# Scatter of the experts' outputs in fp32r with an exact one-hot and a split y, one expert later, and one more weight buffer

## The chip, the cores and the metric

The kernel runs on one core of one Trainium2 chip. The metric is the device time of one execution in microseconds (us); three executions of the kernel before took 1401.58, 1402.41 and 1404.16 us (median 1402.41).

## What is computed

The program is three transformer layers over 256 tokens of 1024 features: a retention layer and a stick-breaking attention layer, each with a gated feed-forward, and then a layer with two mixers and a mixture of experts. The change lies in the last part, cut here to what matters:

```
hn2 = rms_norm(x, g_norm2) * (1 + scale2) + shift2
ffn = hierarchical_moe(hn2, ...)      # 4 groups x 8 experts; top-1 group, top-2 experts in it
#   per expert e, on the tokens routed to it:
#   y = (silu(xb @ w_gate[e]) * (xb @ w_up[e])) @ w_down[e]     # 1024 -> 512 -> 1024
#   out[token] += y_row * weight(token, choice)
x = x + gate2 * ffn
return rms_norm(x, g_final)
```

All is in fp32. The 32 experts' weights are 6 MB each, 192 MB of the 374.68 MB that the program moves.

## The kernel before

**The experts' stage** (`experts`, from 898.60 us of the span to its end) goes over the 32 experts in order. Each expert has 64 slots for tokens. Two experts make a pair: the x of a pair's 128 slots is gathered at once, and the y of its 128 slots is scattered at once. TensorE (PE) does for expert e, in this order:

- `gate_up` (L1717): 32 products of 64 slots, moving 512 weights each; ScalarE (ACT) then takes the silu into `h` (L1721) and VectorE (DVE) multiplies by the up half (L1722).
- `down` of the expert before, e - 1 (L1747): 8 records of products, then the transposes of `h` of expert e (`turn`, L1729), then 8 more. DVE then copies the transposes to `hT` (L1733), which is one buffer that the `down` products still read, and takes y out of PSUM times the layer's gate (L1753), in two halves of 64 partitions, to one half of `Y`.
- where e is odd, `gather` (L1696) of the next pair: one-hot products of x into two PSUM tiles; ACT takes the first four blocks of 128 features to `xg` (L1708), DVE the last four (L1706). The next `gate_up` reads them block by block.
- where e is even and not 0, `sc` of the pair that is then complete (L1832): four full-size fp32 products `accs[t][j] += S[j]^T Y[j]`, S being a [128 slots, 256 tokens] matrix that holds a token's routing weight where the token sits in the slot. S is made on DVE at the start of an odd expert, by `slots` (L1759, L1761), ahead of the one-hot for the gather, `hot` (L1660 to L1667).

In the first expert's turns the last steps of the routing (`route_rest`) are put in between: rows of slot positions and of weights (`rowsb`) come at expert 1, behind the gather.

**The weights' ring.** `Stream` keeps a plan of all 1 MB chunks of weights in the order of their use and issues their DMAs on the SyncE queue (L131) into a ring of buffers; a chunk's DMA is issued as soon as a buffer is released, which PE's last product on the old chunk does. The ring has `RING` = 10 buffers from the start, gets three more of small tiles' memory and others later, and five at the start of the experts' stage. DMAs of constants go by the GpSimd (POOL) queue, which uses a scratch region of SBUF.

**Numbers in fp32r.** Elsewhere in the kernel an fp32 product is made as three fp32r products of split operands; `hilo` (L363, L364; for weights L153, L156) makes such a split: ACT copies to `hi` (rounded to fp32r), DVE subtracts to get `lo`.

Of the kernel before, what the change touches and what calls it, by code (L numbers as in the profile page):

```python
# [21 lines left out]
T = 256  # L22
NT = 2
D = 1024
# [8 lines left out]
RING = 10  # L33
# [9 lines left out]
# the modulation's chunks in the gaps of the first phase and at the four boundaries  # L43
MODS = 6, 5, 5, 6, 10
AHEAD = 6
# the order of the mixers' steps, each with its head or part
# [12 lines left out]
class Blocks:  # L59
    """[:, KC, :] in two tiles of four blocks each."""  # L60
# [12 lines left out]
class Half:  # L73
    """A split half of a chunk; [a:b] gives its (hi, lo) columns, inside a quarter of the chunk."""
# [11 lines left out]
class Stream:  # L86
    """Weights in chunks of up to [128, 2048], in the order of their use; quarters of some are split for fp32r."""
# [11 lines left out]
    def extend(self, pool, tag, bufs, n):  # L99
        """n more buffers, filled before the ones of now come round again."""  # L100
        k = (self.nd - self.at) % len(self.slots)
        self.slots = [(pool, tag, bufs)] * n + self.slots[k:] + self.slots[:k]
        self.at = self.nd
        self.free += n
        self.keep = False
        self.fill()
# [5 lines left out]
    def more(self, n=1):  # L112
        """n of the ring's buffers that had been in use for other things."""
        pool, tag, bufs = self.slots[0]
        self.extend(pool, tag, bufs, n)

    def spare(self):
        """A buffer that no chunk needs any more."""
        assert self.nd >= len(self.plan) and self.free > 0
        t = self.buffer()  # L120
        self.nd += 1
        self.free -= 1
        return t
# [43 lines left out]
    def later(self, *steps):  # L167
        """Steps of other work, one after each quarter that is used."""
        self.todo.extend(steps)
# [7 lines left out]
    def half(self, name):  # L177
        """The next split half."""
# [5 lines left out]
    def chunk(self, name):  # L184
        """The next chunk that is used as it is; release() follows its last use."""
# [8 lines left out]
class Body:  # L194
    # classes of tiles: columns, dtype, and buffers by phase
# [4 lines left out]
    def __init__(self, ctx, tc, a, upto=99):  # L200
# [19 lines left out]
        # small tiles in buffers of the ring, which come to the stream of weights later  # L220
        self.slabs = {}
        for cls, n in (("rot", 2), ("k2", 1)):
            t = [ringp.tile([128, 2048], F32, tag="ring", name="slab", bufs=RING + SLABS) for _ in range(n)]
            self.slabs[cls] = [x[:, o:o + 512] for x in t for o in range(0, 2048, 512)][:6], itertools.count()
            # and 1024 columns more, or all
# [3 lines left out]
    def plan(self):  # L229
# [12 lines left out]
        def bound(i, name, arr):  # L242
            """The modulation's chunks of a boundary with the phase's first one among them."""
# [43 lines left out]
    # ---- tiles  # L287
# [4 lines left out]
    def phase(self, name, **bufs):  # L292
        """A pool for the tiles of a phase, in the place of the last one's."""
# [10 lines left out]
    def view(self, cls, shape, name):  # L304
        """A tile of a class, seen as shape."""
# [19 lines left out]
    def a(self, name="a"):  # L325
        """One of the other four banks."""
        return self.psa.tile([128, 512], F32, tag="a", name=name, bufs=4)

    def banks(self, name):
        """A pool on the four other banks, in the place of the last one's."""  # L330
# [13 lines left out]
    def gain(self, src):  # L344
        """A row of D gains on every partition."""
# [8 lines left out]
    # ---- products  # L354
# [6 lines left out]
    def hilo(self, hi, lo, src):  # L361
        """hi + lo = src, for fp32r."""
# [3 lines left out]
    def transpose4(self, src, c0, name="tr", p=None):  # L366
        """Four blocks of 128 columns of src, transposed."""
# [5 lines left out]
    def natural(self, name, xT, evac):  # L373
        """x @ the next two chunks: [128 tokens, 512] for each tile of tokens."""
# [16 lines left out]
    def transposed(self, name, xT, outs, split=False):  # L391
        """Each out [128 features, 256 tokens] = (x @ the next half)^T; split: tokens of the first tile first."""
# [14 lines left out]
    def rows(self, name, yT, accs, first, last, gate=None, amid=None, begun=None):  # L407
        """accs[t][half] += y[:, two blocks of rows] @ the next chunk; yT[i]: [128, 256] of a block of rows.
        After the last one x gets the sums, and the norm that follows begins; amid: two things on the way;
        begun: the weights of the last one, the first two of their blocks used but for one part."""  # L410
# [55 lines left out]
    def sums1(self, h):  # L466
        """A half of the second tile of tokens of x gets its sums."""
# [3 lines left out]
    # ---- norms  # L471
    def add_x(self, t, h, s, gate=None, square=True):
        """A half of x += s (times a gate), and the sum of its squares."""
# [16 lines left out]
    def rms(self, ss, r=None):  # L490
        """The rms of rows with the sums of squares ss of their halves."""
# [17 lines left out]
    def rsqrt(self, s, n, sign=False, eng=None):  # L509
        """(s / n + EPS) ** -0.5 of one or two columns, on the vector engine alone; negative if sign."""  # L510
# [24 lines left out]
    def to_xT(self, t, h, p, lo):  # L535
        """A half of x^T of a tile of tokens, split: its hi or its lo."""
# [7 lines left out]
    def xT(self):  # L544
        """hi and lo of [128, KC, T]."""
# [4 lines left out]
    def plain_norm(self):  # L550
        """The norm of x that follows some rows: chain(t) after the sums, in steps; join(n) goes on from there,
        on the tensor engine with n products of the modulation."""
# [36 lines left out]
    def boundary(self, i):  # L589
        """The rest of the norm of x, which becomes transposed and split, and products of the modulation."""  # L590
# [14 lines left out]
    # ---- modulation: a quarter of silu(c) @ w_ada + b_ada; rows 32 g of its tile hold 384 columns each  # L605
    def ada(self, i, cls="nat", eng=None):
        """The biases of the quarters that a boundary completes, which get the products."""
# [5 lines left out]
    def ada_steps(self):  # L613
        nc = self.nc
        for s in range(4):
            p = self.w("ada")
            for kc in range(KC):
# [5 lines left out]
                if kc == KC - 1:  # L623
# [3 lines left out]
                    if s == 1:  # L627
                        # by way of memory, for the gate on every partition
# [4 lines left out]
    def ada_columns(self, s, m):  # L633
# [4 lines left out]
        # modc[:, 12 s + 3 g + j] = columns 1536 s + 384 g + 128 j ...  # L638
# [3 lines left out]
    def spread(self, s, t):  # L642
        """t = columns 512 .. 1535 of an odd quarter on every partition."""
# [10 lines left out]
    def setup(self):  # L654
# [22 lines left out]
        for _ in range(WARM):  # L677
            # the tensor engine's clock goes up
            nc.tensor.matmul(p, zero[:, 0:128], zero, start=True, stop=True)
        # the first gain, a row on every partition  # L680
# [45 lines left out]
    # ---- retention  # L726
    def rotary(self, p):
        """The rotated halves of p [128, 512], split."""
# [75 lines left out]
    def conv_taps(self, u, p, cws, n):  # L804
        """u[:, c, :] = the causal convolution of p[:, c T:c T + T] with n taps, the bias last in cws[c]."""
# [9 lines left out]
    # ---- gated feed-forward with the causal convolution  # L815
# [28 lines left out]
    # ---- attention helpers  # L844
    def qk_split(self, b):
        """q / 8 and k of b, split."""
# [9 lines left out]
    # ---- stick-breaking attention  # L856
    def stick(self, xT):
# [20 lines left out]
        def v2(p):  # L878
            """Values of two pairs of heads."""
# [90 lines left out]
    # ---- the second block's mixers  # L970
    def affine(self, out, p, h, A, B, js):
        """out[:, j, :] = a block of p * A + B, by partitions."""
# [8 lines left out]
    def entry_norm(self):  # L981
        """x = the first block's norm of x, x / r * g; then the second block's first norm, modulated: that of x g times
        (mean((x g)^2) + EPS r^2)^-0.5, as r^2 = mean(x^2) + EPS."""
# [20 lines left out]
        def chain(t):  # L1004
            # the squares of x and of x g of both halves, but for the last of these, h
# [15 lines left out]
        def chain0(t):  # L1021
            # Pool has the first half of x g, the other one is there before
# [62 lines left out]
    def halve(self):  # L1085
        """sigmoid(x) = (tanh(x / 2) + 1) / 2"""
# [4 lines left out]
    def mixers(self, xT):  # L1091
# [4 lines left out]
        # of the second tile of tokens; of the first the part from 128  # L1096
# [15 lines left out]
        def gates_post():  # L1112
# [5 lines left out]
            # log_sigmoid(f)  # L1118
# [7 lines left out]
        # a part of vm in the rest of a slab  # L1126
# [23 lines left out]
        def qkm_post(h):  # L1150
            u, s = S.pop(("u", h)), {}

            def silu():
                # u is a half of the convolution: silu = (tanh(u) + 1) u
# [8 lines left out]
            # decays  # L1163
# [85 lines left out]
        def ml3(h, late=False):  # L1249
            """h and its norm over the head."""  # L1250
# [68 lines left out]
        def mo3(i):  # L1319
            """Two heads, transposed."""  # L1320
# [11 lines left out]
        def yt(i):  # L1332
            """Rows of the head and of the pair of heads i, transposed and split."""
# [12 lines left out]
        def wout(i):  # L1346
            if not S.get("accs"):
                S["accs"] = self.accs()
            for j in range(2):
                st.keep = i == 1  # L1350
                self.rows("mix", [[z[:, 2 * i + j, :] for z in yT]], S["accs"], i + j == 0, False)
                if i + j == 2:
                    # the first four blocks of y have been used
# [3 lines left out]
        def begin(k):  # L1357
            """A part of the last rows, their first two blocks."""
# [42 lines left out]
    # ---- experts  # L1401
    def open_experts(self):
        """The experts' tiles take the place of the mixers', and more buffers for weights."""
# [699 lines left out]
```

## Time and profile before

| what | value |
|---|---|
| median of three executions | 1402.41 us |
| the profiled execution: span from its first to its last instruction | 1400.5 us |
| PE busy | 1366.5 us, 98% of the span |
| DVE, ACT, POOL busy | 58%, 43%, 4% |
| granted TensorE clock, mean | 0.996 |
| moved by DMA | 374.68 MB, mean 268 GB/s |
| of it software DMA (POOL's) | 3.54 MB |

The profiled execution's time is known by its span, which lies 1.9 us under the median of the three timed executions. Busy shares are of the whole span; the stages differ (in the experts' stage ACT is at about a tenth and DVE at a third, while the DMA engines are busy all the time), so the prediction reads the stage by itself. A matmul's duration in the profile is longer than the distance to the next one, since matmuls are pipelined; costs on PE are therefore read from distances of starts. An fp32 product is two records; the products of 64 slots run two at a time on halves of the array's columns.

### The profile page before, as it was taken

Reading aid. Unit: us, or ns where it says so; the run is one execution under the profiler, and the core shown is the slowest. Engines: PE = TensorE matmul, PEld = TensorE weight load, DVE = VectorE, ACT = ScalarE, POOL = GpSimd, SP = SyncE. Lnnn points to the kernel's source line nnn. Section 1 sums busy time; section 2 is a strip of 40 time slices with the busy share of each in tenths; the row PEclk is TensorE's granted clock in tenths of the full one; section 3 lists DMA queues with packets and bytes.
Section 4 is the critical chain, followed back from the end, with each engine's and each line's share of the span. In section 5 each row is a group of like instructions: output and inputs, shape, how many; then the busy total and the mean of one; then the engine's idle time right before and its main releaser. Section 6 shows DMA issues by size and latency. Waiting matters only on the chain. (4 is left out here: it accounts for less than half of the span.)

```text
span 1400.5 us, 21543 instructions
## 1 busy us (share of the span) xinstructions
PE 1366.5 (98%) x8332; PEld 999.6 (71%) x8332; DVE 815.8 (58%) x1734; ACT 596.4 (43%) x1187; POOL 60.1 (4%) x117
## 2 busy tenths in 40 slices
PE   9999999999999999999999999999999999999997
PEld 7888878999989998999996898743444334334432
DVE  6767758777775666877777787534233233333323
ACT  5555546566666776666556666410010000000101
POOL 0000000000010001000003122000000000000000
PEclk9999999999999999999999999999999999999999
DMA  9655368544465226654449536899999999999940
GB/s 365 280 186 183 139 235 358 193 184 181 145 257 221 91 76 259 270 183 185 170 143 381 220 128 242 339 398 406 371 411 413 406 416 413 406 403 418 413 183 31
DMA packets 56859, 374.68 MB, mean 268 GB/s; under 512 B 7085, under 2 KB 7905, under 8 KB 15666
## 3 DMA queue, kind: packets, MB, share of 16 engines
q1 hardware_dynamic: 55440, 369.66, 67.8%
q0 software_dynamic: 1168, 3.54, 0.7%
q8 instruction: 66, 1.08, 0.3%
q14 instruction: 39, 0.32, 0.1%
q10 hardware_dynamic: 146, 0.07, 0.0%
HBM read 372.19 MB, written 1.05 MB: 267 GB/s over the span
## 5 line engine op out<-in xcount | busy, mean ns | idle before, releaser
L156 DVE TENSOR_TENSOR lo<-ring,hi 128x512 fp32r<-128x512 f32 x519 | 335.1, 688 | 101.1 <-ACT hi L153 95.2
L153 ACT ACTIVATE hi<-ring 128x512 fp32r<-128x512 f32 x519 | 300.7, 623 | 120.3 <-PE nat_ps L359 41.2
L1717 PE MATMUL gu<-ring,xg 128*64 128x512 f32 x984 | 219.1, 596 | 0.4 <-PEq L1771 0.4
L357 PE MATMUL up<-xT,hi 128*128 128x256 f32 x704 | 199.8, 284 | 0.0
L359 PE MATMUL up<-xT,lo 128*128 128x256 f32 x704 | 199.6, 283 | 0.0
L358 PE MATMUL up<-xT,hi 128*128 128x256 f32 x704 | 199.5, 283 | 0.0
L1721 ACT ACTIVATE h<-gu 64x512 f32<-64x512 f32 x32 | 18.8, 588 | 355.5 <-PE gu L1717 355.5
L1717 PEld LDWEIGHTS gu<-ring,xg 128*64 128x64 f32 x984 | 68.3, 137 | 134.9 <-issue 131.7
L357 PEld LDWEIGHTS up<-xT,hi 128*128 128x128 f32 x704 | 134.2, 191 | 2.0 <-issue 1.2
L358 PEld LDWEIGHTS up<-xT,hi 128*128 128x128 f32 x704 | 134.1, 191 | 0.8
L359 PEld LDWEIGHTS up<-xT,lo 128*128 128x128 f32 x704 | 134.2, 191 | 0.0
L1722 DVE TENSOR_TENSOR h<-h,gu 64x512 f32<-64x512 f32 x32 | 22.1, 691 | 178.0 <-ACT h L1721 178.0
L1747 PE MATMUL y<-ring,hT 128*64 128x512 f32 x480 | 114.7, 599 | 0.5 <-DVE hT L1733 0.5
L812 DVE SCALAR_TENSOR_TENSOR slab<-up,conv,slab 128x254 f32<-128x254 f32 (+1 forms) x176 | 72.7, 476 | 25.7 <-ACT slab L808 25.2
L1832 PE MATMUL acc<-Y,S 128*128 128x512 f32 x128 | 59.2, 606 | 19.3 <-DVE Y L1753 19.3
L1747 PEld LDWEIGHTS y<-ring,hT 128*64 128x64 f32 x480 | 31.7, 136 | 53.6 <-issue 48.1
L357 PE MATMUL nat_ps<-hi,xT 128*128 128x512 f32 x176 | 69.3, 394 | 0.0
L359 PE MATMUL acc<-hi,slab 128*128 128x512 f32 x176 | 69.2, 393 | 0.0
L1696 PEld LDWEIGHTS xg<-goh,x 128*128 128x128 f32 x512 | 60.1, 196 | 12.5 <-issue 12.2
L357 PE MATMUL acc<-hi,slab 128*128 128x512 f32 x176 | 69.0, 392 | 0.0
L358 PE MATMUL acc<-lo,slab 128*128 128x512 f32 x176 | 68.8, 391 | 0.0
L359 PE MATMUL nat_ps<-hi,xT 128*128 128x512 f32 x176 | 68.7, 391 | 0.0
(434 smaller groups left out, 2432.0 us busy)
## 6 DMA issues: line engine op xcount, KB each, us to landing
ring<-gu SPq DMA_DIRECT2D x123, 1024.0 KB, 9.5
ring<-dn SPq DMA_DIRECT2D x59, 1024.0 KB, 8.2
ring<-ffn_u SPq DMA_DIRECT2D x44, 1024.0 KB, 4.8
ring<-ada SPq DMA_DIRECT2D x32, 768.0 KB, 4.4
ring<-ret_w SPq DMA_DIRECT2D x22, 1024.0 KB, 10.3
ring<-ffn_d SPq DMA_DIRECT2D x22, 1024.0 KB, 5.0
ring<-sb SPq DMA_DIRECT2D x12, 1024.0 KB, 6.1
ring<-ret_o SPq DMA_DIRECT2D x8, 1024.0 KB, 7.8
```

The lines of the kernel that those rows point to most:

```text
L153: self.nc.scalar.activation(hi, src, AF.Copy)
L156: (eng or self.nc.vector).tensor_tensor(lo, src, hi.bitcast(F32), op=ALU.subtract)
L357: mm(out, l[0], r[0], start=start, stop=False, **k)
L358: mm(out, l[0], r[1], start=False, stop=False, **k)
L359: mm(out, l[1], r[0], start=False, stop=stop, **k)
L812: nc.vector.scalar_tensor_tensor(u[:, c, s:], p[:, c * T:c * T + T - s], cw[:, n - 1 - s:n - s], u[:, c, s:], op0=ALU.mult, op1=ALU.add)
L1696: self.nc.tensor.matmul(p[:, j * n:j * n + n], self.x[:, t, kc * 128:kc * 128 + 128], oh[:, t, :], start=t + j == 0, stop=t + j == NT + 2, ...
L1717: nc.tensor.matmul(p[64 * i:64 * i + 64, :], xs(kc), raw[:, i * 512:i * 512 + 512], start=kc == 0, stop=kc == KC - 1)
L1721: nc.scalar.activation(h[64:128, :], p[0:64, :], AF.Silu)
L1722: nc.vector.tensor_tensor(h[64:128, :], h[64:128, :], p[64:128, :], op=ALU.mult)
L1747: nc.tensor.matmul(p[64 * i:64 * i + 64, :], hT[:, c, :], raw[:, h * 512:h * 512 + 512], start=c == 0, stop=c == 3)
L1832: nc.tensor.matmul(accs[t][j], S[p][j][:, t * 128:t * 128 + 128], Y[0][:, j, :], start=p == 0, stop=p == E // 2 - 1, skip_group_check=True)
```

## The change

1. `RING` is 11 instead of 10. The memory comes from POOL's DMA scratch, which is set to 2048 bytes of a partition. (Two more things take the rest: a second Y tile, and four S buffers instead of two.)
2. `slot_rows` replaces `scatter_rows` for the pairs: S becomes the exact one-hot (1 where the token sits in the slot) in fp32r, and the slot's weight goes into a column `ws`, [128, 1], summed up by the first operation's accumulator. That is three DVE operations for each S where there were two.
3. y comes out of PSUM times the slot's weight and times the gate into `f` (a `scalar_tensor_tensor`), and `hilo` splits `f` into `Yh` and `Yl`, both fp32r. This happens in each of the two halves: a DVE operation, an ACT copy, a DVE subtraction.
4. `sc` is eight fp32r products (hi and lo for each of four) in the place of four fp32 ones.
5. `sc(q - 1)` comes in the odd expert after the pair, between its `gate_up` and the `down` of the even expert; before, it stood one expert earlier, behind the `down` that completed the pair. The last `sc` stays at the end.
6. At expert 1 the two steps of the routing that make `rowsb`, and the first `slots`, come ahead of the first `down`, as its evacuation needs `ws`.

```diff
-RING = 10
+RING = 11
+SCRATCH = 2048
...
     def down(self, hT, chunks, odd, evac, mid=None):
...
         for i in (odd, 1 - odd):
-            out = outs[i]
             r, h = slice(64 * i, 64 * i + 64), i ^ odd
-            nc.vector.tensor_tensor(out, p[r, :], self.gate2[r, h * 512:h * 512 + 512], op=ALU.mult)
+            evac(i, r, h, p[r, :])
...
+    def slot_rows(self, idx):
+        V, rows, wts = self.nc.vector, *self.rowsb
+        u = self.mp.tile([128, 2 * T], F32, tag="k2", name="su", bufs=2)
+        w = self.mp.tile([128, 1], F32, tag="ws", name="ws", bufs=4)
+        V.scalar_tensor_tensor(u, rows, idx, wts, op0=ALU.is_equal, op1=ALU.mult, accum_out=w)
+        v = self.mp.tile([128, T], F32, tag="k2", name="sv", bufs=2)
+        V.tensor_scalar(v, rows[:, T:], idx, None, op0=ALU.is_equal)
+        s = self.mp.tile([128, T], F32R, tag="S", name="S", bufs=4)
+        V.scalar_tensor_tensor(s, rows[:, 0:T], idx, v, op0=ALU.is_equal, op1=ALU.add)
+        return s, w
...
         def dn(e, mid=None):
...
-                Y[0] = mp.tile([128, 2, 512], F32, tag="Y", name="Y", bufs=1)
-            self.down(hTs.pop(e), stream("dn"), o, [Y[0][0:64, o, :], Y[0][64:128, 1 - o, :]], mid)
+                Y[e // 2] = [mp.tile([128, 2, 512], F32R, tag=n, name="Y" + x, bufs=1) for n, x in (("Y", "h"), ("Yl", "l"))]
+            hi, lo = Y[e // 2]
+            def evac(i, r, h, p):
+                f = mp.tile([128, 512], F32, tag="k2", name="y", bufs=2)
+                nc.vector.scalar_tensor_tensor(f[r, :], p, S[e // 2][h][1][r, :], self.gate2[r, h * 512:h * 512 + 512],
+                                               op0=ALU.mult, op1=ALU.mult)
+                self.hilo(hi[r, h, :], lo[r, h, :], f[r, :])
+            self.down(hTs.pop(e), stream("dn"), o, evac, mid)
         def sc(p):
+            ys, ss = Y.pop(p), S.pop(p)
             for t in range(NT):
                 for j in range(2):
-                    nc.tensor.matmul(accs[t][j], S[p][j][:, t * 128:t * 128 + 128], Y[0][:, j, :], start=p == 0,
-                                     stop=p == E // 2 - 1, skip_group_check=True)
+                    for i, y in enumerate(ys):
+                        nc.tensor.matmul(accs[t][j], ss[j][0][:, t * 128:t * 128 + 128], y[:, j, :], start=p + i == 0,
+                                         stop=p == E // 2 - 1 and i == 1, skip_group_check=True)
...
+            if e > 1 and odd:
+                sc(q - 1)
+            if e == 1:
+                next(rest)
+                next(rest)
+                slots(0)
             if e:
                 dn(e - 1, turn)
...
-            if e and not odd:
-                sc(q - 1)
...
-    nc = bacc.Bacc("TRN2", target_bir_lowering=False, num_devices=1)
+    nc = bacc.Bacc("TRN2", target_bir_lowering=False, num_devices=1, dynamic_dma_scratch_size=SCRATCH)
```

How the order moves on two engines. Line numbers of the changed kernel are one higher up to the changed functions and more behind them (L1718 is `gate_up`, L1748 `down`, L1859 `sc`). First PE, in a pair in the middle of the stage. Before, from the `down` of an odd expert to the gather of the next pair:

```order
L1747 MATMUL y<-ring,hT 64x512 x4
L1729 MATMUL hT<-ident,h 128x64 x4
L1747 MATMUL y<-ring,hT 64x512 x4
L1832 MATMUL acc<-Y,S 128x512 x4
L1717 MATMUL gu<-ring,xg 64x512 x16
L1747 MATMUL y<-xa,hT 64x512 x4
L1729 MATMUL hT<-ident,h 128x64 x4
L1747 MATMUL y<-ring,hT 64x512 x4
L1696 MATMUL xg<-goh,x 128x128 x16
```

The same place now, up to the first two products of the scatter, and then from the last of its eight on:

```order
L1748 MATMUL y<-ring,hT 64x512 x4
L1730 MATMUL hT<-ident,h 128x64 x4
L1748 MATMUL y<-ring,hT 64x512 x4
L1718 MATMUL gu<-ring,xg 64x512 x16
L1859 MATMUL acc<-Yh,S 128x512
L1859 MATMUL acc<-Yl,S 128x512
```

```order
L1859 MATMUL acc<-Yl,S 128x512
L1748 MATMUL y<-ring,hT 64x512 x4
L1730 MATMUL hT<-ident,h 128x64 x4
L1748 MATMUL y<-ring,hT 64x512 x4
L1697 MATMUL xg<-goh,x 128x128 x16
L1718 MATMUL gu<-xa,xg 64x512 x4
```

The scatter has moved behind a whole `gate_up`, and stands ahead of the `down` whose y goes into the same Y tiles. Then DVE, in an odd expert, from the multiplication of `h` over the evacuation of y to the one of the gathered x. Before:

```order
L1722 TENSOR_TENSOR h<-h,gu 64x512
L1733 COPY hT<-hT 128x256
L1753 TENSOR_TENSOR Y<-y,gate_10392 64x512 x2
L1706 TENSOR_SCALAR xg<-xg,A_10085,modc 128x128 x4
L1722 TENSOR_TENSOR h<-h,gu 64x512
```

Now (between the two operations of each half, ACT makes `Yh`, and its two `Yh` stand ahead of its four operations on the gathered x):

```order
L1723 TENSOR_TENSOR h<-h,gu 64x512
L1734 COPY hT<-hT 128x256
L1848 SCALAR_TENSOR_TENSOR y<-y,ws,gate_10394 64x512
L365 TENSOR_TENSOR Yl<-y,Yh 64x512
L1848 SCALAR_TENSOR_TENSOR y<-y,ws,gate_10394 64x512
L365 TENSOR_TENSOR Yl<-y,Yh 64x512
L1707 TENSOR_SCALAR xg<-xg,A_10087,modc 128x128 x4
L1723 TENSOR_TENSOR h<-h,gu 64x512
```

The evacuation of y has become a chain over two engines, and the gathered x waits behind it on both.

## Rows read from the trace of the kernel before

**Rows 1.** The page, part 1: engine, busy us, share of the span, instructions.

```profile
PE 1366.5 (98%) x8332; PEld 999.6 (71%) x8332; DVE 815.8 (58%) x1734; ACT 596.4 (43%) x1187; POOL 60.1 (4%) x117
```

**Rows 2.** Waits, 960 to 1340 us: who waited for whom, us, times, longest.

```profile
PE acc L1832 <- DVE Y L1753: 16.0, 13, 1.2
...
PEld y L1747 <- DMA ring<-gu: 2.6, 9, 0.3
```

**Rows 3.** Waits of the SyncE queue, 900 to 1400 us.

```profile
SPq L131 <- PE gu L1717: 292.8, 116, 13.8
```

**Rows 4.** Timeline of one pair: start us, us, engine, line, count, [idle before <-releaser].

```profile
1184.94 0.42 DVE L1733 COPY hT<-hT 128x256 f32<-128x256 f32 x1 [2.66 <-PE y L1747]
1185.37 1.41 DVE L1753 TENSOR_TENSOR Y<-y,gate 64x512 f32<-64x512 f32 x2
...
1186.12 3.70 PE L1832 MATMUL acc<-Y,S 128*128 128x512 f32 x8 [1.23 <-DVE Y L1753]
...
1189.75 7.09 PE L1717 MATMUL gu<-ring,xg 128*64 128x512 f32 x32
...
1196.67 1.89 PE L1747 MATMUL y<-xa,hT 128*64 128x512 f32 x8
...
1198.49 0.46 PE L1729 MATMUL hT<-ident,h 64*128 64x64 f32 x4
...
1200.74 3.84 PE L1696 MATMUL xg<-goh,x 128*128 128x128 f32 x32
...
1202.89 1.51 ACT L1708 ACTIVATE xg<-xg,modc,A 128x128 f32<-128x128 f32 x4 [5.42 <-PE xg L1696]
1204.51 7.09 PE L1717 MATMUL gu<-ring,xg 128*64 128x512 f32 x32
```

**Rows 5.** Timeline of an earlier stage: fp32r products of 512 columns, back to back.

```profile
402.57 0.39 PE L359 MATMUL acc<-hi,slab 128*128 128x512 f32 x1
...
402.80 0.40 PE L357 MATMUL acc<-hi,slab 128*128 128x512 f32 x1
```

**Rows 6.** Timeline of the mixers: fp32r products right behind fp32 transposes.

```profile
863.05 0.49 PE L357 MATMUL acc<-hi,xT 128*128 128x512 f32 x1
...
863.38 0.40 PE L358 MATMUL acc<-lo,xT 128*128 128x512 f32 x1
```

**Rows 7.** DVE groups by line and form, 880 to 1400 us: busy us, mean ns.

```profile
L1759 DVE SCALAR_TENSOR_TENSOR su<-posr,early,wtr 128x512 f32<-128x512 f32 x32 | 23.7, 741 | 1.2 <-ACT wtr L1652 1.0
...
L1706 DVE TENSOR_SCALAR xg<-xg,A,modc 128x128 f32<-128x128 f32 x64 | 21.9, 404 | 30.9 <-PE xg L1696 30.9
L1665 DVE TENSOR_SCALAR goh<-early,pq,rx 128x128 f32<-128x128 f32 x60 | 16.7, 343 | 0.5
L1761 DVE TENSOR_TENSOR S<-su 128x256 f32<-128x256 f32 x32 | 13.6, 425 | 22.6 <-PE acc L1832 20.9
```

**Rows 8.** The page, part 5: the splits of weights on DVE and ACT.

```profile
L156 DVE TENSOR_TENSOR lo<-ring,hi 128x512 fp32r<-128x512 f32 x519 | 335.1, 688 | 101.1 <-ACT hi L153 95.2
L153 ACT ACTIVATE hi<-ring 128x512 fp32r<-128x512 f32 x519 | 300.7, 623 | 120.3 <-PE nat_ps L359 41.2
```

**Rows 9.** Timeline of the first expert.

```profile
897.82 1.50 ACT L1708 ACTIVATE xg<-xg,modc,A 128x128 f32<-128x128 f32 x4 [4.76 <-PE xg L1696]
898.60 7.09 PE L1717 MATMUL gu<-ring,xg 128*64 128x512 f32 x32
```

**Rows 10.** Timeline of the last expert.

```profile
1385.94 3.65 PE L1747 MATMUL y<-ring,hT 128*64 128x512 f32 x16 [0.53 <-DVE hT L1733]
...
1390.39 3.70 PE L1832 MATMUL acc<-Y,S 128*128 128x512 f32 x8 [0.80 <-DVE Y L1753]
```

**Rows 11.** Two windows: us, busy of PE, PEld, DVE, ACT, (POOL); clock, DMA share, GB/s.

```profile
1210.00:1220.00 10.00, 8.77 (x36) 3.11 (x32) 3.46 (x6) 0.59 (x1) 0.00 (x0) 1.00 1.01 424
...
1350.00:1360.00 10.00, 10.00 (x64) 5.66 (x62) 3.86 (x8) 2.09 (x5) 0.00 (x0) 1.00 0.01 2
```

**Rows 12.** DMA issues of the whole span: KB each, median us to landing.

```profile
gain<-ffn_norm POOLq DMA_DIRECT2D x2, 512.0 KB, 10.4
```

More of the change, by code (lines that the diff above doesn't have):

```diff
@@ L1734, in h_T, with down @@
         return hT
-    def down(self, hT, chunks, odd, outs, mid=None):
+    def down(self, hT, chunks, odd, evac, mid=None):
         nc = self.nc
@@ L1759, in scatter_rows @@
         nc.vector.scalar_tensor_tensor(u, rows, idx, wts, op0=ALU.is_equal, op1=ALU.mult)
-        s = self.mp.tile([128, T], F32, tag="S", name=name, bufs=2)
+        s = self.mp.tile([128, T], F32, tag="S", name=name, bufs=4)
         nc.vector.tensor_tensor(s, u[:, 0:T], u[:, T:], op=ALU.add)
         return s
+    def slot_rows(self, idx):
[8 more added lines that the diff above has]
+        return s, w
     def overflow(self, accs):
@@ L1783, in overflow, with times_gate @@
                 h = self.gate_up(lambda kc: xg[:, kc, :], loads(a["gu"]))
-                self.down(self.h_T(h, hT), loads(a["dn"]), 0, [y[0:64, :], y[64:128, :]])
+                def times_gate(i, r, h, p):
+                    nc.vector.tensor_tensor(y[r, :], p, self.gate2[r, h * 512:h * 512 + 512], op=ALU.mult)
+                self.down(self.h_T(h, hT), loads(a["dn"]), 0, times_gate)
                 self.spread_rows(rows, self.xpos)
@@ L1819, in slots @@
         def slots(p):
-            S[p] = [self.scatter_rows(self.rc["slot"][:, j * 16 + p:j * 16 + p + 1], *self.rowsb, "S")
-                    for j in range(2)]
+            S[p] = [self.slot_rows(self.rc["slot"][:, j * 16 + p:j * 16 + p + 1]) for j in range(2)]
         def dn(e, mid=None):
@@ L1869, in experts @@
                 xg[q + 1] = self.gather(oh.pop(q + 1), 128)
-            if e and not odd:
-                sc(q - 1)
             if e == 6:
                 add_x()
-            for _ in range(2 if e == 1 else 1 if e else 0):
+            if e > 1:
                 next(rest, None)
-            if e == 1:
-                slots(0)
             if e == E - 2:
```

## Prediction

> **What bounds the kernel now.** I read the page's first part, then the waits of the experts' stage, then one pair of experts on the timeline. PE is busy for 98% of the span [rows 1], so the first question is who it waits for in the rest. Between 960 and 1340 us PE's only wait of size is that of the scatter for Y, 13 times, never over 1.2 us; what it waits for weights comes to 0.3 us at a time [rows 2]. The SyncE queue, in turn, spends 292.8 us waiting until a `gate_up` has released a buffer [rows 3]. So the ring is full, the transfers follow PE and not the other way round, although the DMA engines are busy all the time (share 1.01 at 424 GB/s, [rows 11]). The stage is bound by PE's own work plus that one wait, and time is saved there by shorter or fewer products, if no new wait comes.
>
> One pair, read off [rows 4]: `gate_up` of the odd expert from 1189.75 to 1196.67, 6.92 us; `down` with the transposes to 1200.74, 4.07; gather to 1204.51, 3.77. The even expert has the same `gate_up` and `down`; then comes the scatter. The last `down` product ends where DVE's copy of `hT` begins, 1184.94; the next `gate_up` begins at 1189.75: 4.81 us, of which 1.23 is the wait for Y, and the rest four fp32 products with a second, shorter wait between them. The pair takes 30.6 us (two times 6.92 and 4.07, 3.77, 4.81).
>
> **The change, part by part.**
>
> *The products of the scatter.* Eight fp32r products of 512 columns take the place of four fp32 ones. Each shows a duration of 0.39 us, but back to back the starts are 0.23 apart (402.57 to 402.80, [rows 5]). A change from fp32 to fp32r costs a little: the second product there started 0.33 after the first (863.05 to 863.38, [rows 6]). So 0.33 + 7 x 0.23 = 1.94 us. The bounds are 8 x 0.23 = 1.84 and 8 x 0.39 = 3.12, if they did not overlap; I take 1.94, since the rows are of the same form, with weights that change each time.
>
> [...]
>
> *The wait.* The scatter now stands behind a `gate_up` of 6.92 us. Its operands are ready when the evacuation is: the copy of `hT` first (0.42, [rows 4]), then for each half f, hi, lo. For f I take 0.74, the same operation from SBUF [rows 7], for hi 0.62, for lo 0.69 [rows 8] (rows of 128 partitions, taken for 64 too), for each hand-over between engines 0.04, an estimate from the scatter's start 0.05 after the first Y half (1185.37 + 0.70 to 1186.12, [rows 4]). From the end of `down`: copy to 0.47, f 1.21, hi 1.87, lo 2.60, f 3.34, hi 4.00, lo 4.73. That is before 6.92, so the wait goes, with 2.2 us to spare. Parts one and two together: 4.81 - 1.94 = 2.87 us for each of the 15 scatters inside the loop, 43.0 us.
>
> *What is late next: the gathered x.* In an odd expert the same chain follows `down`, and on ACT the two hi stand ahead of its four operations on the gathered x. Those began 2.15 us after the `down` had ended (1202.89 - 1200.74, [rows 4]) and now cannot before 4.00. One takes 0.46 of the four's 1.51 (they overlap), so the first block is ready at 4.50, while PE is through with the gather at 3.77. `gate_up` starts with a first block alone: in the first expert it started at 898.60, while ACT worked on the four from 897.82 to 899.32 [rows 9]. So a new wait of 4.50 - 3.77 = 0.7 us in each of 15 gathers, 10.5 us. Later blocks come every 0.35 us against two product pairs each on PE, and DVE's blocks (from 4.73 on, 4 operations of up to 0.40, [rows 7]) by 6.3, needed 3.5 us into the `gate_up`. Bounds: 0 if the chain is 0.7 shorter, 1.8 if the `gate_up` needed all four.
>
> *What else is queued behind the chain on DVE.* In the even expert's wake: two `slot_rows` at three operations, one-hot for the gather, then `h` of the odd expert. From 4.73: two times (0.74 + 0.1 for the accumulator's read + about 0.4 + 0.43) [rows 7] to 8.1 (L1759 and L1761; the 256 columns in the middle are put a little above the 343 ns of L1665's 128); a short subtraction and four one-hots at 0.28 (16.7/60, [rows 7]) and an addition of 0.43 to 9.8; `h` multiplied by 10.5. PE wants it for the transposes at 6.92 + 1.94 + 1.82 (1196.67 to 1198.49, [rows 4]) = 10.7. So it is just in time: zero, bounds 0 and 0.5 us a pair. The cover is the scatter's 1.94; were it shorter, this wait would appear.
>
> *The end.* The last `down` no longer has an idle DVE before it: the evacuation of expert 30 lasts until 4.73 after that `down`, and the one of expert 31 adds 4.2 behind it. So the last lo comes at 9.0, and five products remain, ending at about 10.3. Before, the last `down` began at 1385.94, 0.5 after the one before it had ended, and the scatter ended at 1394.09, 8.6 after [rows 10]. The norm's squares on ACT then start behind later sums, which are closer together than their 0.8 us each. I take +2.5 us, bounds 1.7 and 3.
>
> *The ring's eleventh buffer, POOL's scratch, the steps moved at expert 1.* The ring is full and PE waits for no weights [rows 2, 3], so one more buffer changes no time. POOL's DMAs, with less scratch, could be later; the nearest row is a landing time of 10.4 us [rows 12], and PE's waits show none of them: zero, bounds 0 and 10 us once. At expert 1 the same products stand in another order; DVE has `gate_up`'s time for the slots.
>
> The sum against the profiled span: 1400.5 - 43.0 + 10.5 + 2.5 = 1370.5 us; the median of the runs lies 1.9 above the span, so **1372 us**, 2.2% less.
>
> *Can the transfers follow?* The pair would take 30.6 - 2.87 + 0.7 = 28.4 us for 12 chunks of 1.05 MB, 443 GB/s, more than the 424 of the best window. But all weights have landed by 1350 [rows 11], and the last are used from 1385.94 on [rows 10], 36 us later. The use comes about 30 us earlier, so even unmoved transfers would be in time, and they move too, as their buffers come free earlier.
>
> **The rivals.**
>
> *Half of it is lost in the chain or in unpipelined products.* Either the eight products cost 3.12 (1.2 x 15 = 18 us more), or `gate_up` waits for all four blocks (1.1 x 15 = 17 more). Time 1389 to 1390. For it: a chain over two engines that no row shows in this place. Against: [rows 5] and [rows 9].
>
> *Transfers bind, and nothing is gained.* The DMA share of 1.01 in the stage [rows 11] says that no engine of theirs has time left; if the weights' last landing and PE's last product were tied, the time would stay at 1402. For it: 424 GB/s is the top of all windows. Against: waits of 0.3 us, and the 36 us of lead. [...]
>
> *Slower: hand-overs.* The chain has three between DVE and ACT ahead of the gathered x, and lo is one more ahead of `h`. If they make the chain longer by x, the `gate_up` waits x longer in the even expert, and the transposes of `h` x - 0.2 in the odd one. The gain of a pair, 2.87 - 0.7 = 2.17, is gone at x = 1.2 us, a chain of 5.9 us instead of 4.73. At x = 2 the time is 1372 + 15 x (2 + 1.8) = 1429. For it: DVE and ACT are both in order, and one late operation holds all behind it. Against: the hand-over of 0.05 in [rows 4], which would have to be six times as long and more.
>
> That the change doesn't do what it says can be left out: the order of the instructions shows the eight products and their place.
>
> **How the numbers follow.** Forecast, 1361 to 1380 us: 0.74. Half lost, 1380 to 1399: 0.12. Transfers bind: 0.06. Slower: 0.08. A measurement of this kernel can tell some 0.2% from no change, 2.8 us. Faster 0.74 + 0.12 = 0.86, within it 0.06, slower 0.08. The lower end is the sum without the new wait at the gather, 1372 - 10.5 = 1361. The upper one takes in the wait at twice its size (+10.5) and a third of a microsecond a pair at the transposes (+5), 1388; what lies above that is the rest of the half-lost case and the last two, some 0.2.
>
> **What would show it.** Right: the scatter's eight products in about 1.9 us with no wait before them; `gate_up` of even experts waiting about 0.7 us for ACT's first block; transposes of `h` without a wait of size; 28.4 us a pair; a longer end by 2 to 3 us; the SyncE queue still waiting for PE, if for shorter. Wrong: products 0.39 apart, a wait of PE for `ring`, or waits before the transposes or gathered x of over 1.2 us.

## The result, and the profile of the changed kernel

| | before | after |
|---|---|---|
| median | 1401.99 us (4 runs, 1401.41 to 1404.16) | 1387.79 us (4 runs, 1386.61 to 1390.00) |
| ratio, 95% interval | | 0.9894 (0.9880 to 0.9908) |
| span of the profiled execution | 1400.5 us | 1384.5 us |
| granted TensorE clock, mean | 0.996 | 0.991 |

The change is faster by 14.2 us, 1.1%. Forecast were 30: the direction is right, the size half. The spans differ by 16.0 us. Cut where PE starts a gather, the difference splits as follows (us):

| stretch | before | after | difference | forecast |
|---|---|---|---|---|
| start to the gather in expert 1 | 918.99 | 918.70 | -0.3 | 0 |
| 14 pairs, to the gather in expert 29 | 435.18 | 410.37 | -24.8 | -30.4 |
| from there to the end | 46.3 | 55.4 | +9.1 | +0.3 |

In the first line two things cancel. The first `gate_up` starts 2.4 earlier (896.19 against 898.60), which the second run below puts down to scatter; from there to the gather in expert 1 it is 22.51 where it was 20.39, as the products of the moved routing steps (item 6) now stand ahead of that gather. Their 1.9 us are gone from the next pair, so the -24.8 contains them. The loop thus gave 5.6 us less than forecast, 7.5 without the moved products, and the end took 9 us back. The profile after, first the page's first line; against [rows 1] PE's share is a point lower, and DVE and ACT have the longer chain to do:

```profile
PE 1346.3 (97%) x8332; PEld 998.1 (72%) x8332; DVE 874.1 (63%) x1862; ACT 636.2 (46%) x1251; POOL 60.1 (4%) x117
```

PE's waits from 896 to 1384 us (who waited for whom, us, times, longest); the scatter's wait for Y of [rows 2] is not among them, and none is for a ring buffer:

```profile
PE gu L1718 <- ACT xg L1709: 13.1, 15, 0.9
PE gu L1718 <- DVEq L1783: 5.6, 1, 5.6
PE hT L1730 <- DVE h L1723: 3.4, 2, 1.9
PE acc L1859 <- ACT Yh L364: 2.7, 2, 2.1
...
```

The timeline of a steady pair, with the same columns as [rows 4]:

```profile
1207.90 0.50 PE L1859 MATMUL acc<-Yh,S 128*128 128x512 f32 x1
...
1208.24 0.40 PE L1859 MATMUL acc<-Yl,S 128*128 128x512 f32 x1
...
1208.48 0.39 PE L1859 MATMUL acc<-Yh,S 128*128 128x512 f32 x1
...
1209.94 1.94 PE L1748 MATMUL y<-ring,hT 128*64 128x512 f32 x8
...
1214.07 3.84 PE L1697 MATMUL xg<-goh,x 128*128 128x128 f32 x32
1214.19 0.42 DVE L1734 COPY hT<-hT 128x256 f32<-128x256 f32 x1 [2.95 <-PE y L1748]
...
1217.63 0.63 ACT L364 ACTIVATE Yh<-y 64x512 fp32r<-64x512 f32 x1 [1.52 <-DVE y L1848]
1218.28 1.50 ACT L1709 ACTIVATE xg<-xg,modc,A 128x128 f32<-128x128 f32 x4
...
1218.79 1.51 PE L1718 MATMUL gu<-ring,xg 128*64 128x512 f32 x6 [0.89 <-ACT xg L1709]
```

The scatter takes 2.04 us (1207.90 to 1209.94) where 1.94 were forecast, and waits for nothing: its products start 0.34, then 0.23 apart, as [rows 5, 6] had them. The second `Yh` ends 4.19 after `down` (1218.26 - 1214.07; forecast 4.00), and `gate_up` waits 0.89 for ACT's first block (forecast 0.7). A steady pair takes 28.75 us instead of 30.69: 1.94 less, where 2.17 were forecast.

Two places of the loop did worse, experts 3 and 5. Expert 3 on the timeline; DVE works on the routing's `cnt` to `inc` from 939.03 to 942.27, and only then on the slots, the one-hot and `h` (at expert 5 the routing ahead of the slots takes 2.2 us, 970.41 to 972.57, and PE waits 1.53):

```profile
942.19 0.74 DVE L1769 SCALAR_TENSOR_TENSOR su<-posr,early,wtr 128x512 f32<-128x512 f32 x1
...
946.91 0.69 DVE L1723 TENSOR_TENSOR h<-h,gu 64x512 f32<-64x512 f32 x1
947.66 0.46 PE L1730 MATMUL hT<-ident,h 64*128 64x64 f32 x4 [1.86 <-DVE h L1723]
```

The end, on the timeline and then in windows (us, busy of PE, PEld, DVE, ACT, POOL; clock, DMA share, GB/s):

```profile
1344.91 0.42 DVE L1734 COPY hT<-hT 128x256 f32<-128x256 f32 x1 [2.61 <-PE y L1748]
...
1348.95 0.68 DVE L365 TENSOR_TENSOR Yl<-y,Yh 64x512 fp32r<-64x512 f32 x1 [0.70 <-ACT Yh L364]
...
1350.49 9.80 PE L1718 MATMUL gu<-ring,xg 128*64 128x512 f32 x32 [5.63 <-DVEq L1783]
...
1372.71 0.51 PE L1859 MATMUL acc<-Yh,S 128*128 128x512 f32 x1 [2.07 <-ACT Yh L364]
...
1377.03 0.63 PE L1859 MATMUL acc<-Yh,S 128*128 128x512 f32 x1
1377.46 0.63 PE L1859 MATMUL acc<-Yl,S 128*128 128x512 f32 x1
```

```profile
1350.00:1360.00 10.00, 9.51 (x32) 3.14 (x32) 2.93 (x8) 0.00 (x0) 0.00 (x0) 0.70 0.00 0
...
1370.00:1380.00 10.00, 5.16 (x12) 2.25 (x8) 6.93 (x15) 5.80 (x15) 0.00 (x0) 0.65 0.07 26
```

L1782 and L1783 belong to `overflow`, the block for tokens past an expert's 64 slots: every engine loads a count from `tabi`, and a `tc.If` skips the block, as here there are none. The block stands behind `down` of expert 29. When PE, ACT and DVE took the branch (length in ns, start in us; PE's sequencer is listed as PEld):

```profile
L1783 PEldq COMPARE_BRANCH  x1: 378/378/378, 1343.6 to 1343.6; - x1
...
L1783 ACTq COMPARE_BRANCH  x1: 45/45/45, 1349.3 to 1349.3; - x1
...
L1783 DVEq COMPARE_BRANCH  x1: 76/76/76, 1350.1 to 1350.1; - x1
```

PE itself branched at 1343.6, before its `down` had ended. It waits behind the block: the first product of `gate_up` is released by DVE's passing of L1783 (`<-DVEq L1783`), and DVE comes to its branch only when it is through with the evacuation (the last `Yl` ends at 1349.63). So the block is a barrier between PE and whatever DVE has in hand. Before, DVE branched at 1370.2, as the scatter began, and the scatter, which stood between the `down` and the block, had waited for the evacuation in any case. The block cost PE 0.41 us there:

```profile
1374.35 7.09 PE L1717 MATMUL gu<-ring,xg 128*64 128x512 f32 x32 [0.41 <-PEq L1771]
```

Now the scatter has gone ahead of that `down`, PE has nothing between the `down` and the `gate_up` behind the block, and waits there for the whole chain: 5.63 us. Behind it the clock is 0.70 in 1350 to 1360, and `gate_up` of expert 31 takes 9.80 us where 7.09 is the rule. Last, from the end of the first of the two final `down` to the end of the span it is 18.0 us (1366.49 to 1384.50) where it was 15.07; some of that is the clock too (0.50 from 1375 to 1378), as the last products start 0.43 apart. Together 5.2 + 2.7 + 2.9 = 10.9, less the 1.8 of this pair's scatter and gather: +9.1.

### The profile page after: what moved, and what is told of

It reads as the page before. It is cut to its first block, busy times and chain, and to the rows that moved or that the text cites. A ratio compares the mean times of both kernels' runs of the same rounds, so it can differ in the third digit from the quotient of the medians.

```text
span 1384.5 us, 21682 instructions
## 1 busy us (share of the span) xinstructions
PE 1346.3 (97%) x8332; PEld 998.1 (72%) x8332; DVE 874.1 (63%) x1862; ACT 636.2 (46%) x1251; POOL 60.1 (4%) x117
## 5 line engine op out<-in xcount | busy, mean ns | idle before, releaser
L1718 PE MATMUL gu<-ring,xg 128*64 128x512 f32 x976 | 219.0, 600 | 17.0 <-ACT xg L1709 11.3
L1718 PEld LDWEIGHTS gu<-ring,xg 128*64 128x64 f32 x976 | 69.4, 138 | 152.1 <-issue 120.8
L364 ACT ACTIVATE Yh<-y 64x512 fp32r<-64x512 f32 x64 | 40.2, 628 | 212.2 <-DVE y L1848 212.2
L1748 PE MATMUL y<-ring,hT 128*64 128x512 f32 x488 | 117.2, 602 | 0.5 <-DVE hT L1734 0.5
L365 DVE TENSOR_TENSOR Yl<-y,Yh 64x512 fp32r<-64x512 f32 x64 | 43.9, 686 | 45.3 <-ACT Yh L364 45.3
```

Source lines behind the costliest of these rows:

```text
L364: self.nc.scalar.activation(hi, src, AF.Copy)
L365: self.nc.vector.tensor_tensor(lo, src, hi.bitcast(F32), op=ALU.subtract)
L1718: nc.tensor.matmul(p[64 * i:64 * i + 64, :], xs(kc), raw[:, i * 512:i * 512 + 512], start=kc == 0, stop=kc == KC - 1)
L1748: nc.tensor.matmul(p[64 * i:64 * i + 64, :], hT[:, c, :], raw[:, h * 512:h * 512 + 512], start=c == 0, stop=c == 3)
```

## The experiments

**Theory.** The gain in the loop is real, about 1.9 a pair. What is missing sits in four places: the block's barrier with the clock behind it (8 us), the wait at the gather (0.95 in each of 15, where 0.7 were forecast), `h` of experts 3 and 5 behind the routing (3.4), the final chain (2.9, where 2.5 were forecast). **Rivals:** the stream of weights binds (at 417 GB/s in 1000 to 1300 us); the buffer or the scratch does something (in the profiled executions the changed kernel starts its first `gate_up` 2.4 us earlier, 896.19 against 898.60); the fp32r products cost more than they seem.

**The buffer taken out of the change.**

```diff
-RING = 11
+RING = 10
```

> The changed kernel with 10 ring buffers in place of 11. Theory (the transfers do not bind in either kernel; the lost time sits at the control-flow block of expert 30, in the clock behind it and in the final chain): within 2 us of the changed kernel's 1387.8. Rival 1 (the weight stream has become the bound, and the buffer is what still feeds it): slower by 5 to 15 us, 1393 to 1403, with waits of the gate_up products for a ring buffer of over 0.4 us each. Rival 2 (the 2.4 us that the changed kernel is ahead of the one before when the experts begin come from the buffer): 1390 and the experts' first product again near 898.6 in place of 896.2.

Measured 1387.44 us (ratio to before 0.9901, 0.9884 to 0.9918), `gate_up`'s waits the same to 0.1 us in total and none for a buffer. Its first `gate_up` starts at 896.68, with 10 buffers as early as with 11. The theory holds.

**The buffer alone in the kernel before**, with the scratch at 2048.

```diff
-RING = 10
+RING = 11
+SCRATCH = 2048
```

> The kernel before with 11 ring buffers and the small scratch, nothing else changed. Theory: the buffer alone changes nothing in the experts' loop, 1400 to 1403. Rival 2: it brings what the changed kernel is ahead when the experts begin, 1399.5, with the experts' first product near 896.2. Rival 1 (the stream binds): 1390 to 1398.

Measured 1402.61 (1.0004, 0.9994 to 1.0013): nothing. Its first `gate_up` starts at 896.04, but over all kernels profiled here it starts between 896.68 and 898.83 with 10 buffers and between 896.04 and 900.04 with 11. So the 2.4 us are no more than the scatter from one profile to the next, and the rival on the buffer falls.

**Without `overflow`**, in both kernels; the block for further tokens is left out.

```diff
-                self.overflow(accs)
```

> The changed kernel without the block for tokens past the 64 slots of an expert (left out: what would be computed for such tokens). Theory: TensorE's idle time of 5.63 us at that block falls to under 0.5, and the gate_up of expert 31 is back from 9.80 to about 7.1 as the clock has no cause to fall: 8 us less, 1379 to 1381. Rival (the idle time is the scatter's and the evacuations', and only moves to the next product that waits for them; the clock falls anyway as the last experts come to their end): 0 to 3 us less, 1385 to 1388.

> The same block left out of the kernel before, the control of the run above. Theory: its engines had all come to rest where the block stands, behind the scatter, and TensorE waited 0.41 us there: 0 to 1 us less, 1401 to 1402. Rival (the block costs some 5 us wherever it stands): 1396 to 1398.

Measured 1380.29 for the changed kernel (0.9847, 0.9831 to 0.9864), 7.5 less, and 1401.26 for the one before (0.9996, 0.9986 to 1.0005). Expert 31 in the changed kernel without the block:

```profile
1345.04 7.04 PE L1718 MATMUL gu<-ring,xg 128*64 128x512 f32 x32
```

Neither wait nor slow products, at a clock of 1.00 in that window. The same block costs 7.5 us in the one kernel and at most 2 in the other.

What it costs in the changed kernel is the work of DVE that it makes PE wait for, 5.63 us, with the slower `gate_up` behind that; in the kernel before PE stood 0.41 us there.

**The fp32r products without the move**, the scatter back behind the `down` that completes the pair.

```diff
-            if e > 1 and odd:
-                sc(q - 1)
...
+            if e and not odd:
+                sc(q - 1)
```

> The changed kernel with the scatter put back behind the down that completes the pair: the fp32r products and the chain of the evacuation without the move. Theory: the chain is 4.73 us long from the end of down (copy, then f, hi, lo, f, hi, lo), so the scatter ends 5.8 after down where it took 4.81 in the kernel before, the gather's wait of 0.9 stays, the block at expert 30 costs nothing again: 15 x (1.0 + 0.95) = 29 us slower than before, 1426 to 1434. Rival (the fp32r products are cheap enough by themselves): 1398 to 1405, with a scatter of 4.8 or less. Rival (they are no cheaper than the fp32 ones): 1440 and more.

Measured 1457.78 (1.0402, 1.0385 to 1.0420): slower as the theory says, but by 56 us, not 29. The scatter on PE's timeline, and two windows of 3 us (clock is the third number from the end):

```profile
1218.23 0.50 PE L1859 MATMUL acc<-Yh,S 128*128 128x512 f32 x1 [1.97 <-ACT Yh L364]
1218.96 0.49 PE L1859 MATMUL acc<-Yl,S 128*128 128x512 f32 x1 [0.22 <-DVE Yl L365]
1220.39 0.78 PE L1859 MATMUL acc<-Yh,S 128*128 128x512 f32 x1 [0.94 <-ACT Yh L364]
1221.11 0.79 PE L1859 MATMUL acc<-Yl,S 128*128 128x512 f32 x1
1221.70 0.63 PE L1859 MATMUL acc<-Yh,S 128*128 128x512 f32 x1
1222.13 0.63 PE L1859 MATMUL acc<-Yl,S 128*128 128x512 f32 x1
```

```profile
1216.00:1219.00 3.00, 0.81 (x4) 0.23 (x2) 1.94 (x4) 0.63 (x1) 0.00 (x0) 1.00 1.01 429
1219.00:1222.00 3.00, 2.06 (x4) 1.21 (x5) 2.30 (x5) 0.63 (x1) 0.00 (x0) 0.74 1.01 429
1222.00:1225.00 3.00, 3.00 (x10) 1.27 (x11) 2.90 (x10) 0.00 (x0) 0.00 (x0) 0.69 0.97 407
```

PE stands still for 1.97, 0.22 and 0.94 us in the chain, and then the clock falls: the last products start 0.43 apart instead of 0.23, where the granted clock is 0.74 and 0.69 (the windows from 1219 to 1225). From `down` to the next `gate_up` it is 7.2 us (1216.31 to 1223.54), 1.4 more than expected, and a steady pair takes 34.13. The waits are the same in every pair: from 960 to 1400 us PE waits for `Yh` 26 times, 37.8 us in all, 13 times this pair's 2.91. Of the 27 us of the miss some 20 are the clock, which I had left at 1.00 throughout the loop: about 1.2 in the last products and 0.14 in the `gate_up` behind them (7.06 to the next start, where 6.92 is the rule), in each of 15 pairs, an estimate from this one. The rest was not taken apart.

That the clock falls in every pair fits its mean, 0.95 in each 100 us from 1000 to 1400: the two windows above lose 1.7 us of clock, 5% of a pair. It falls behind waits for an evacuation, none over 1.97 us here.

**The move without the fp32r products**: the kernel before with four S buffers and `sc(q - 1)` behind the odd expert's `gate_up`; the memory comes from the scratch.

```diff
+            if e > 1 and odd:
+                sc(q - 1)
             if e:
                 dn(e - 1, turn)
...
-            if e and not odd:
-                sc(q - 1)
```

> The kernel before with the scatter moved behind the next gate_up and nothing of fp32r: the move without the chain (four S buffers need memory, taken from the scratch of the dynamic DMA). Theory: the wait of 1.23 and the shorter one between the products go, the four fp32 products take about 3.5 in place of 4.81: 1.3 us less for each of 15 pairs, no wait at the gather, 2 to 6 us given back at the block of expert 30: 1384 to 1389, about as fast as the whole change. Rival (the gain of the change comes from the fp32r products): 1396 to 1402.

Measured 1385.38 (0.9890, 0.9874 to 0.9907): as fast as the whole change. From its PE timeline:

```profile
1210.30 3.70 PE L1833 MATMUL acc<-Y,S 128*128 128x512 f32 x8
1213.92 1.94 PE L1748 MATMUL y<-ring,hT 128*64 128x512 f32 x8
...
1221.82 7.09 PE L1718 MATMUL gu<-ring,xg 128*64 128x512 f32 x32
...
1352.60 7.09 PE L1718 MATMUL gu<-ring,xg 128*64 128x512 f32 x32 [2.19 <-DVEq L1772]
```

The fp32 scatter without its waits is 3.62 us (1210.30 to 1213.92), the pair 29.38: 1.31 less than before. Nothing waits at the gather, as the evacuation is one DVE operation a half. At the block PE waits only 2.19 (the short evacuation), and the `gate_up` behind it keeps its clock. So the fp32r part of the change is worth 0.63 a steady pair (29.38 to 28.75): 8.8 us over the 14 pairs, less the 3.4 of waits at experts 3 and 5, which the move alone does not have. The longer chain gives more than that back at the end: 55.4 us from the gather in expert 29 on, where the move alone has 46.9.

**The evacuation in two parts, gathered x between them**: both f first, then the gather and its ACT operations, then the splits.

```diff
-                self.hilo(hi[r, h, :], lo[r, h, :], f[r, :])
+                late.append((hi[r, h, :], lo[r, h, :], f[r, :]))
...
+        late = []
...
+        def split():
+            while late:
+                self.hilo(*late.pop(0))
...
                 xg[q + 1] = self.gather(oh.pop(q + 1), 128)
+            split()
...
         dn(E - 1)
+        split()
```

> The changed kernel with the evacuation cut in two: both f first, the split into hi and lo only behind the gathered x. Theory: PE's wait for ACT's gathered x, 0.9 in each of 15 pairs, goes (14 us); where no gather stands between, the order f, f, hi, hi, lo, lo makes the chain some 1.4 shorter, which the transposes of experts 3 and 5 and the block of expert 30 get back (up to 4): 1368 to 1374, pairs of 27.8. Rival (PE waits for DVE's blocks of x or for the buffers of f instead): 1383 to 1390. Rival (the stream now binds, as a pair of 27.8 asks for 453 GB/s and the best window shows 424): 1375 to 1383, with waits for ring buffers.

Measured 1366.69 (0.9754, 0.9737 to 0.9770), a little below the expected band: a steady pair is 27.80, and PE waits for nothing between 960 and 1310 us.

**The same order without the gather between**: `split()` right behind both f, so f, f, hi, hi, lo, lo.

> The changed kernel with the evacuation in the order f, f, hi, hi, lo, lo, nothing put behind the gathered x. Theory (the wait at the gather is there only because the second hi on ACT waits for the second f, and that on DVE for the first lo): hi, hi end 2.5 after down, ACT's first block of x is ready at 3.0, before the gather's end at 3.77, so pairs of 27.8 and 1366 to 1369, as with x ahead of the split. Rival (any work of the split ahead of x on ACT makes PE wait): 1372 to 1380, with a wait of 0.3 to 0.6 in each pair.

Measured 1367.24 (0.9749, 0.9729 to 0.9769). An odd expert on the timeline, `down` having ended at 1289.09:

```profile
1289.66 1.53 DVE L1848 SCALAR_TENSOR_TENSOR y<-y,ws,gate 64x512 f32<-64x512 f32 x2
...
1290.50 1.35 ACT L364 ACTIVATE Yh<-y 64x512 fp32r<-64x512 f32 x2 [6.83 <-DVE y L1848]
1291.22 1.40 DVE L365 TENSOR_TENSOR Yl<-y,Yh 64x512 fp32r<-64x512 f32 x2
1291.88 1.51 ACT L1709 ACTIVATE xg<-xg,modc,A 128x128 f32<-128x128 f32 x4
...
1292.85 1.94 PE L1718 MATMUL gu<-xa,xg 128*64 128x512 f32 x8
```

DVE and ACT now overlap: the two `Yh` end 2.76 after `down` (1291.85) instead of 4.19, and x is there before PE asks for it. So it is the order of six operations, not their number, that made PE wait: in the change's order the second f stands on DVE behind the first lo, which waits for ACT (0.76 us in the steady pair above), so that it starts at 1216.84 where the first f had ended at 1215.38; and ACT, idle for 1.52 us, takes up the gathered x only behind the second `Yh` (1218.28). The order is worth 20.5 us: 15 x 0.95 = 14.3 at the gathers and 3.2 behind the start of the last `gate_up`, the rest at experts 3 and 5 (0.7 of waits instead of 3.4) and at the block (4.3 instead of 5.6).

**The routing's last steps at odd experts only.**

```diff
-            if e > 1:
+            if e > 1 and odd:
                 next(rest, None)
```

> The changed kernel with the last steps of the routing taken at the ends of odd experts, so that none stands on DVE ahead of the slots of experts 3 and 5. Theory: PE's waits for h at experts 3 and 5 go, 3.6 us less: 1383.5 to 1385. Rival (the slots alone make h late there): 1387 to 1388.5.

Measured 1383.26 (0.9867, 0.9851 to 0.9884), 4.5 less, a little below the expected band; the two waits that went are 3.4 of it. The transposes of expert 3 follow `down` at once there:

```profile
946.28 1.94 PE L1748 MATMUL y<-ring,hT 128*64 128x512 f32 x8
948.15 0.46 PE L1730 MATMUL hT<-ident,h 64*128 64x64 f32 x4
```

**The block at expert 31**, behind `gate_up` and the scatter, in the changed kernel and in the one with the move alone. Its tiles get a tag of their own, as `h` is pending there; in the changed kernel their memory is that of one ring buffer, so `RING` is 10 (which by itself changed nothing, above). The edit of the changed kernel, without the tags:

```diff
-RING = 11
+RING = 10
...
-            if last:
-                self.table("sqrt")
...
+            if last:
+                self.overflow(accs)
+                self.table("sqrt")
             if e == 1:
...
-                self.overflow(accs)
```

> The changed kernel with the block for further tokens kept, but moved to expert 31, behind gate_up and the scatter, where the evacuation of y is long over (its tiles get a tag of their own, as h is pending there, in the memory of one ring buffer: RING 10). Theory: the block then costs what it did in the kernel before, some 0.4 us, and the clock does not fall ahead of the gate_up: 1379 to 1382, as without the block. Rival (the block costs 5 us wherever PE would otherwise go on): 1386 to 1388.

> The kernel before with the scatter moved (fp32, no split) and the block of further tokens moved to expert 31 in the same way. Theory: its wait of 2.19 at the block falls to about 0.4: 1382.5 to 1384.5. Rival (it does not matter there): 1385 to 1386.

Measured 1381.13 (0.9853, 0.9833 to 0.9873), as without the block, and 1383.19 (0.9873, 0.9852 to 0.9893). PE's product behind the block in the first of them, and in the second:

```profile
1356.89 1.94 PE L1748 MATMUL y<-ring,hT 128*64 128x512 f32 x8 [0.46 <-DVEq L1783]
```

```profile
1361.54 1.94 PE L1748 MATMUL y<-ring,hT 128*64 128x512 f32 x8 [0.30 <-PEq L1772]
```

**All three mends together** (f, f, hi, hi, lo, lo; routing; block at expert 31), with `RING` 10 as in the run before.

> The three mends together: the order f, f, hi, hi, lo, lo, the routing's steps at odd experts, the block at expert 31. Theory: from 1366 to 1369 of the order alone another 4.0 of PE's wait at the block, 1.7 of the slower gate_up behind it and 1 at experts 3 and 5 go: 1359 to 1363, below both kernels. Rival (the stream of weights, at its top rate of 424 GB/s, holds the rest up): 1363 to 1368 with PE waiting for ring buffers.

Measured 1360.12 us (0.9702, 0.9684 to 0.9721; 1359.82 to 1360.49): 3% under the kernel before and 28 us under the change. PE's waits from 960 us on are all at the end, and the SyncE queue shows how near the transfers have come:

```profile
PE acc L1866 <- ACT Yh L364: 1.5, 1, 1.5
PE y L1748 <- DVE hT L1734: 0.5, 1, 0.5
PE y L1748 <- DVEq L1783: 0.4, 1, 0.4
PE acc L1866 <- DVE Yl L365: 0.3, 1, 0.3
```

```profile
SPq L132 <- PE gu L1718: 127.7, 67, 13.9
SPq L132 <- DMA ring<-gu: 112.3, 56, 3.0
SPq L132 <- DMA ring<-dn: 57.3, 28, 2.1
```

The queue waits for `gate_up` less than half as long as in [rows 3], and 170 us for transfers, where the kernel before shows no such wait. The last weights land at about 1332 (the window 1330 to 1340 moves 106 GB/s, a quarter of the rate) and the last `down` begins at 1343.09: 11 us of lead. Read in the same way (247 GB/s from 1340 to 1350) the kernel before had 40; the prediction's 36 took 1350 for the landing. By this a still faster PE would meet the transfers soon, which no run here shows.

## Why the prediction was half right

- **The products of the scatter, 1.94 us: right.** 2.04 measured, with starts as in the rows that it was taken from.
- **The wait for Y, 1.23 gone: right.** The scatter waits for nothing in the loop. The pair of the last kernel, 27.80, is 2.89 under the one before; the prediction had 2.87 for these two parts.
- **The gathered x, 0.7 us: right in kind, mis-sized.** 0.89 measured, as the chain up to the second `Yh` took 4.19 and not 4.00; the hand-overs were 0.01 to 0.12 rather than 0.04. With the scatter's 0.1 the pair gained 1.94 instead of 2.17, some 3.5 of the 14 us by which the span missed the sum.
- **`h` "just in time", zero: wrong at two experts.** In a steady pair it holds. At experts 3 and 5, where DVE has 3.2 and 2.2 us of routing ahead of the slots, it does not, and PE waited 1.86 and 1.53. I had worked out the queue on DVE from a pair in the middle of the stage; the pairs at its start have more in it. The routing moved away gave 4.5.
- **"The end", +2.5: the step that failed.** The final chain took 2.9, within its bounds, with a part of the clock in it that the prediction did not have: the last lo came 9.0 after the `down`, as forecast, the last product ended about 11.4 after it and not 10.3. What failed is that the sum has no term for the block ahead of the chain: it was put at nothing, without a reason and without a word. It cost 5.2 us of barrier and 2.7 of clock; taken out or moved, 7.5 and 6.7 us came back. The trace of before shows the block at 0.41, which is what it costs behind the scatter's own wait for the same evacuation, and the change took that cover away.
- **The ring's buffer, the scratch: zero, right.** Both ways round the times stay. The steps moved at expert 1 take 2.1 us ahead of the gather and give 1.9 back behind it, so that zero holds too.
- **Transfers bind: wrong, as argued.** From 1000 to 1300 us the DMA share is 1.00 or 1.01 in all kernels between 1360 and 1402 us, while the rate rose from 406 to 421 GB/s as PE got faster; the differences between the kernels lie in PE's waits, products and clock as far as they were taken apart.

The rival "half of it is lost", 1389 to 1390, comes nearest in time, but for the wrong reasons: neither unpipelined products (the starts are 0.23 apart) nor a wait for all four blocks (0.89 us, for the first) is in the trace.

## What to carry to other kernels

A step that moves on one engine uncovers what stood behind it: list every barrier, control-flow block and routing step that comes after its old place, and price each anew without it. Where an evacuation goes over two engines in several operations, issue it stage by stage (f, f, hi, hi, lo, lo) and not half by half; here that one change of order was worth more than the change itself (20.5 us against 14.2). And test the parts alone: the move by itself gave all of the change's gain (1385.38 us against 1387.79), and the cheaper products paid only once their longer chain was out of the way (1367.24).

## What was not expected of the hardware

The granted clock was lower behind some short idle times of PE. With 1.97, 0.22 and 0.94 us of waiting inside one scatter it was 0.74 and 0.69 in the 6 us from 1219 on (the fp32r products without the move). Behind a wait of 5.63 us at the block it was 0.70 in the next 10 us, and `gate_up` took 9.80 us instead of 7.09; behind one of 4.42 it was 0.83 from 1333 to 1343, and `gate_up` took 8.78 (the evacuation in two parts). The final scatter shows both cases: with waits of 2.07, 0.22 and 0.64 us its last products start 0.43 apart at a clock of 0.50 (the changed kernel), with waits of 1.52 and 0.34 they start 0.23 to 0.24 apart (the evacuation in two parts). Behind a single wait of 2.19 us (the move alone) the clock was 1.00 from 1350 to 1360, and behind the 1.23 of the kernel before 1.00 from 1210 to 1220. What decides between these was not tried.
